# A SwiGLU feed-forward in token rows: stationary activations, streamed weights, and 32x32 turns before the down product

## The chip, the cores and the metric

The kernel runs on one core of a Trainium2 chip. The metric is the device time of one execution in microseconds; three runs of the kernel before took 2255.55, 2255.99 and 2256.78 us, so the median is 2255.99.

## The reference

One residual block on 256 tokens of width 2048, all in float32: a half-step feed-forward (FFN1), a token-mixing part (forgetting attention, differential attention, memory attention, merged by gates), and a second half-step feed-forward (FFN2). Each part has an RMSNorm in front and one behind. The change touches the two feed-forwards alone:

```python
def rmsnorm(x, g):
    y = x * lax.rsqrt(jnp.mean(x * x, axis=-1, keepdims=True) + EPS)
    return y * g

def swiglu(h, w_gate, w_up, w_down):          # h: 256 x 2048
    return (jax.nn.silu(h @ w_gate) * (h @ w_up)) @ w_down   # 2048 -> 5632 -> 2048

h = rmsnorm(x, ffn1_pre_g)
x = x + 0.5 * rmsnorm(swiglu(h, ffn1_w_gate, ffn1_w_up, ffn1_w_down), ffn1_post_g)
...  # token mixing
h = rmsnorm(x, ffn2_pre_g)
x = x + 0.5 * rmsnorm(swiglu(h, ffn2_w_gate, ffn2_w_up, ffn2_w_down), ffn2_post_g)
```

## The kernel before

**Split operands.** Each float32 operand of a large product is split into hi (rounded to the float32r format) and lo (what is left), and the product is taken as hi*hi + hi*lo + lo*hi. Activations are split once and kept as a tile with index (k, hi or lo, token), k counting slices of 128 rows. `rows_of` makes such tiles; its offset argument shifts the start by some elements. The factor of the norm per token is not applied to h: it is applied behind the product.

**The weight stream.** Class `Stream` lists all weight pieces of the kernel in the order of their use. A raw tile is 1 MB, loaded by one DMA on SP's queue (line 69), three raw buffers. Half of a raw tile is one piece; its hi comes from a ScalarE cast (line 92), its lo from a VectorE subtraction (line 93), into four split buffers. `ahead` splits as many pieces as there are free buffers, and issues the loads that follow; `take` hands out pieces (and splits them if nobody did so before); `release` gives their buffers back. The order of the instructions on each engine is the order of the program: nothing reorders it, so a wait holds up all that is behind it on that engine.

**Two forms of product.** `mm_a` (lines 206, 208) holds 128x128 blocks of weights stationary and streams activations: a matmul of 512 columns (hi weights against hi and lo of 256 tokens) and one of 256 (lo weights against hi). The result has FF features on partitions, and its two halves are added by `lr_sum` (lines 403, 405). `mm_b` (lines 247 to 249) holds 128x128 blocks of activations stationary and streams 512 columns of weights, three matmuls per slice and per token tile t of 128 tokens. The result has tokens on partitions.

**The feed-forward before.** `ffn_up` runs over 44 blocks m of 128 FF features. Block 0 takes gate and up together (`proj_a2`), with turns of later parts of x put in between; all others take `proj_a` for gate, then for up. Then the block is finished in eight to ten short instructions of 128x256: `lr_sum`, a multiplication by the row of token factors (`times_row`, a row that `row_of` spreads over the partitions), Silu, again the row, `lr_sum` of up, the product, and the split into `gh` (lines 282, 283), which is already in the layout that the down product wants as its stationary operand. The down product (`PostProj.body` and `last`) uses `proj_b`, which runs `mm_b` over pieces with two banks, one per token tile.

**PSUM.** Four banks are used in turn for products, four for transposes and attention.

**The ends of FFN1 and FFN2's beginning.** At the start x is loaded in four parts of 512 columns, each transposed on TensorE (`transpose_to`, lines 320 to 330), scaled by the norm's gain and split into `hT1`. Ahead of FFN2 the last product of the mixing part ends with token tile 0 first: with `lag=7` tile 0 is finished, x updated and turned (`x2_in`) while tile 1's last seven pieces run. Tile 1's update (line 397) and turns follow, and then FFN2's first block.

Of the kernel before, what the change touches and what calls it, by code (L numbers as in the profile page):

```python
# [16 lines left out]
P = 128  # L17
# [3 lines left out]
FF = 5632  # L21
FT = FF // P
NB = 428
NBS = 448
# [12 lines left out]
class Stream:  # L37
# [33 lines left out]
    def ahead(self, most=8):  # L71

        for _ in range(most):
            if self.done == len(self.plan):
                break
            _, r, half, extra = self.plan[self.done]
            if extra:
                if self.extra_pool is None:
                    break
                pool, tag = self.extra_pool, "x"  # L80
            else:
                if sum(not p[3] for p in self.plan[self.used:self.done]) == self.split_bufs:
# [8 lines left out]
            for i in range(2) if self.done == 0 else (slice(0, 2),):  # L91
# [24 lines left out]
def tile_block(ctx, tc, x, mem, f1gu, f1d, wqk, wv, wmkv, wgate, wbr, wout, f2gu, f2d,  # L116
# [21 lines left out]
    st = Stream(nc, rawp, splitp, 3, 4)  # L138
    st.add("gu1", f1gu[0, 0], f1gu[1, 0])
    for m in range(1, FT):  # L140
        st.add("gate1", f1gu[0, m])
        st.add("up1", f1gu[1, m])
    for i in range(4 * 11):
# [13 lines left out]
    for i in range(16):  # L157
        st.add("out", wout[i], extra={12: (1,), 13: (0, 1)}.get(i, ()))
    st.add("gu2", f2gu[0, 0], f2gu[1, 0])
    for m in range(1, FT):  # L160
        st.add("gate2", f2gu[0, m])
        st.add("up2", f2gu[1, m])
    for i in range(4 * 11):
# [46 lines left out]
    def new_bank(name):  # L210
        return mmp.tile([P, 512], F32, tag="mm", name=name)
# [12 lines left out]

    def proj_a2(name, act, inserts=()):

        banks = [new_bank("mm_a2") for _ in range(2)]
        inserts = dict(inserts)
        for half in range(2):
            ws = st.take(name, 2)  # L230
            for kk in range(8):
                k = half * 8 + kk
                inserts.get(k, lambda: None)()
                for i in range(2):
                    mm_a(banks[i], ws[i], kk, act, k, k == 0, k == KT - 1)
            st.release(2)
        return banks

    def mm_b(bank, piece, w, act, t, k0, start, stop):
# [10 lines left out]

    def proj_b(name, act, nk, w, banks=None, start=True, stop=True, lag=0, first_done=None, inserts=()):


        if banks is None:
            banks = [new_bank("mm_b") for _ in range(2)]
        pieces = nk // 2
        for i in range(pieces - lag):
            st.ahead()
            p, = st.take(name)
            for t in range(2):  # L260
                mm_b(banks[t], p, w, act, t, 2 * i, start and i == 0, stop and i == pieces - 1)
            st.release()
            fill()
        if lag:
# [12 lines left out]
        return banks  # L277

# [65 lines left out]
    class PostProj:  # L344
# [23 lines left out]

        def body(self):
            for n in range(3):  # L370
                banks = proj_b(self.name, self.act, self.nk, 512)
                for t in range(2):
                    self.evac(n, t, banks[t])
                self.load_g(n + 1)
# [39 lines left out]

    def ffn_up(idx, hT, stats, setup, inserts=()):

        first = []
        for m in range(FT):
            bu = None
            if m == 0:  # L420
                bg, bu = proj_a2(f"gu{idx}", hT, inserts)
                stats()
                first.append(proj_a(f"gate{idx}", hT))
                row, tp, gh = setup()
            else:
                bg = first.pop() if first else proj_a(f"gate{idx}", hT)
            ga = tp.tile([P, S], F32, tag="ga", name="ga", bufs=1)
            lr_sum(ga, bg, tp)
            times_row(ga, row)
            sg = tp.tile([P, S], F32, tag="sg", name="sg", bufs=1)  # L430
            nc.scalar.activation(out=sg, in_=ga, func=AF.Silu)
            times_row(sg, row)
            if bu is None:
                bu = proj_a(f"up{idx}", hT)
            up = tp.tile([P, S], F32, tag="ga", name="up", bufs=1)
            lr_sum(up, bu, tp)
            nc.vector.tensor_tensor(out=up, in0=sg, in1=up, op=ALU.mult)
            split_to(gh[:, m, 0], gh[:, m, 1], up)
        return gh

# [3 lines left out]
    hpool = h1_stack.enter_context(tc.tile_pool(name="hT1", bufs=1, side="right", reuse_waits="tile"))  # L444
    tp1 = h1_stack.enter_context(tc.tile_pool(name="ft1", bufs=1, side="right", reuse_waits="tile"))
    gp1 = g1_stack.enter_context(tc.tile_pool(name="gh1", bufs=1, side="left", reuse_waits="tile"))
    hT1 = rows_of(hpool, KT, OFF, name="hT1")
    gh1 = rows_of(gp1, FT, 0, name="gh1")
# [15 lines left out]
    def x_in(c):  # L464
        for t in range(2):
            transpose_to(hT1, chunk(x_sb, t, c), t, 4 * c, C_G1 + 4 * c, tp1)()

    x_in(0)
    st.ahead(2)

    xr = []
    ffn_up(1, hT1, lambda: xr.extend(token_rstd(x_sb, t) for t in range(2)), lambda: (row_of(xr, hpool), tp1, gh1),
           {1: lambda: x_in(1), 3: lambda: st.ahead(1), 5: lambda: x_in(2), 7: lambda: st.ahead(1),
            8: lambda: x_in(3), 10: lambda: st.ahead(2)})
    h1_stack.close()
# [427 lines left out]

    h3T = rows_of(h2p, KT, OFF, tag="h", name="h3T")
    fg_stack = ExitStack()
# [20 lines left out]
    post2.update(1, 1)  # L926
    splits = [x2_in(1, 0, 2), x2_in(1, 1)]

    def turn(c):
        splits.append(x2_in(1, c))  # L930

    splits.pop(0)()

    g2_stack, tp2_stack = ExitStack(), ExitStack()

    def setup2():
        row = row_of(h3r, h2p)
        fg_stack.close()
        mg_stack.close()
        yb_stack.close()  # L940
        tp = tp2_stack.enter_context(tc.tile_pool(name="ft2", bufs=1, side="left", reuse_waits="tile"))
        gp = g2_stack.enter_context(tc.tile_pool(name="gh2", bufs=1, side="right", reuse_waits="tile"))
        return row, tp, rows_of(gp, FT, 0, name="gh2")

    gh2 = ffn_up(2, h3T, lambda: h3r.extend(token_rstd(x_sb, t) for t in range(2)), setup2,
                 {1: lambda: (splits.pop(0)(), post2.update(1, 2), st.ahead(1)), 2: lambda: (turn(2), post2.update(1, 3)),
                  4: lambda: (splits.pop(0)(), st.ahead(1)), 5: lambda: turn(3), 8: lambda: splits.pop(0)(),
                  10: lambda: st.ahead(2)})
    tp2_stack.close()
    h2_stack.close()  # L950
    with tc.tile_pool(name="fg2", bufs=1, side="left", reuse_waits="tile") as fgp:
# [7 lines left out]

        post3.body()  # L960
        banks = post3.last(lag=4, first_done=lambda bank: finish(0, bank))
# [83 lines left out]
```

## Time and profile before

| what | value |
|---|---|
| median of three runs | 2255.99 us |
| the profiled execution | 2256.76 us |
| span of that execution, first to last instruction | 2255.0 us |
| TensorE (PE) busy | 99% |
| weight loads into TensorE (PEld) | 86% |
| VectorE (DVE) busy | 62% |
| ScalarE (ACT) busy | 49% |
| DMA engines, mean share of the main queue | 53.0% |
| mean granted TensorE clock | 0.998 |

A busy share is the time in which an engine had an instruction in it. Matmuls overlap in their ends, so the time from one start to the next is shorter than the duration that the profile gives: what a matmul costs in a stream is read from the starts.

### The profile page before, as it was taken

To read this page: it belongs to the slowest core of one execution; us is meant where nothing else is said; L and a number is where in the kernel's file an instruction comes from. 1 tells how busy PE (TensorE), PEld (TensorE's weight loads), DVE (VectorE), ACT (ScalarE), POOL (GpSimd) and SP (SyncE) were. 2 spreads that over 40 slices of the span, in tenths; PEclk is the share of its full clock that TensorE was granted. 3 is DMA by queue.
4 is the path that set the end of the run, shared out by engine and by line. 5 is a ranking of instruction groups with operands and counts; after the bars stand their busy time and mean duration, and the time that the engine had idled before them with its cause. 6 is when DMAs were issued, how large, how long until landed. Compare 5 with 4: busy or idle time off the path is not lost. (4 is left out here: it accounts for less than half of the span.)

```text
span 2255.0 us, 30353 instructions
## 1 busy us (share of the span) xinstructions
PE 2235.5 (99%) x12028; PEld 1947.3 (86%) x12028; DVE 1408.1 (62%) x1969; ACT 1097.8 (49%) x1704; POOL 11.3 (1%) x22
## 2 busy tenths in 40 slices
PE   8999999999999999999999999999999999999998
PEld 7888888888888898888888888878888888888887
DVE  6666666665444756766776767566666666664444
ACT  6444544445444654444555555456544445544433
POOL 0000000000000000000000000000000000000000
PEclk9999999999999999999999999999999999999999
DMA  6555555556555454544555555545555555555553
GB/s 226 190 194 194 189 187 187 190 192 229 191 202 199 171 190 148 180 144 159 174 181 205 176 199 187 208 154 197 187 187 189 192 194 191 187 199 203 192 202 138
DMA packets 63646, 423.15 MB, mean 188 GB/s; under 512 B 7440, under 2 KB 7824, under 8 KB 16144
## 3 DMA queue, kind: packets, MB, share of 16 engines
q1 hardware_dynamic: 59616, 415.33, 53.0%
q10 hardware_dynamic: 3888, 5.88, 0.8%
q8 instruction: 94, 1.54, 0.3%
q14 instruction: 48, 0.39, 0.1%
HBM read 419.09 MB, written 2.10 MB: 187 GB/s over the span
## 5 line engine op out<-in xcount | busy, mean ns | idle before, releaser
L93 DVE TENSOR_TENSOR lo<-raw,hi 128x1024 fp32r<-128x1024 f32 (+2 forms) x793 | 943.1, 1211 | 453.1 <-ACT hi L92 450.6
L92 ACT CAST hi<-raw 128x1024 fp32r<-128x1024 f32 (+2 forms) x793 | 808.7, 1037 | 382.3 <-PE mm_b L249 307.9
L206 PE MATMUL mm_a<-hT,hi 128*128 128x512 f32 x1408 | 490.7, 391 | 2.9 <-DVE hT L330 2.9
L206 PE MATMUL mm_a<-h3T,hi 128*128 128x512 f32 x1408 | 491.0, 392 | 1.0 <-DVE h3T L330 1.0
L208 PE MATMUL mm_a<-hT,lo 128*128 128x256 f32 x1408 | 398.3, 283 | 1.1 <-DVE lo L93 1.1
L208 PE MATMUL mm_a<-h3T,lo 128*128 128x256 f32 x1408 | 398.0, 283 | 0.0
L206 PE MATMUL mm_a<-h2T,hi 128*128 128x512 f32 x1088 | 384.0, 394 | 0.0
L206 PEld LDWEIGHTS mm_a<-hT,hi 128*128 128x128 f32 x1408 | 265.3, 188 | 58.8 <-ACT hi L92 3.5
L206 PEld LDWEIGHTS mm_a<-h3T,hi 128*128 128x128 f32 x1408 | 265.5, 189 | 56.8 <-ACT tg L322 1.2
L208 PE MATMUL mm_a<-h2T,lo 128*128 128x256 f32 x1088 | 306.5, 282 | 0.0
L403 ACT ACTIVATE left<-mm_a 128x256 f32<-128x256 f32 x244 | 93.5, 383 | 378.3 <-PE mm_a L208 378.3
L247 PE MATMUL mm_b<-hi,gh 128*128 128x512 f32 x704 | 274.2, 390 | 0.0
L249 PE MATMUL mm_b<-hi,gh 128*128 128x512 f32 x704 | 273.9, 389 | 0.0
L248 PE MATMUL mm_b<-lo,gh 128*128 128x512 f32 x704 | 273.9, 389 | 0.0
L208 PEld LDWEIGHTS mm_a<-hT,lo 128*128 128x128 f32 x1408 | 267.0, 190 | 2.5 <-DVE lo L93 2.5
L208 PEld LDWEIGHTS mm_a<-h3T,lo 128*128 128x128 f32 x1408 | 267.2, 190 | 0.0
L206 PEld LDWEIGHTS mm_a<-h2T,hi 128*128 128x128 f32 x1088 | 204.4, 188 | 41.9
L208 PEld LDWEIGHTS mm_a<-h2T,lo 128*128 128x128 f32 x1088 | 205.7, 189 | 0.2
L249 PEld LDWEIGHTS mm_b<-hi,gh 128*128 128x128 f32 x704 | 132.1, 188 | 27.6
L247 PEld LDWEIGHTS mm_b<-hi,gh 128*128 128x128 f32 x704 | 132.1, 188 | 27.4
L248 PEld LDWEIGHTS mm_b<-lo,gh 128*128 128x128 f32 x704 | 132.2, 188 | 27.1
L405 DVE TENSOR_TENSOR up<-mm_a,left 128x256 f32<-128x256 f32 x88 | 37.4, 424 | 71.4 <-ACT left L403 71.4
(205 smaller groups left out, 1779.5 us busy)
## 6 DMA issues: line engine op xcount, KB each, us to landing
raw<-in_f2gu SPq DMA_DIRECT2D x88, 1024.0 KB, 4.8
raw<-in_f1gu SPq DMA_DIRECT2D x86, 1024.0 KB, 4.8
raw<-in_wgate SPq DMA_DIRECT2D x48, 1024.0 KB, 4.7
raw<-in_f1d SPq DMA_DIRECT2D x44, 1024.0 KB, 4.8
raw<-in_f2d SPq DMA_DIRECT2D x44, 1024.0 KB, 4.7
raw<-in_wv SPq DMA_DIRECT2D x24, 856.0 KB, 4.5
raw<-in_wqk SPq DMA_DIRECT2D x20, 1024.0 KB, 4.8
raw<-in_wbr SPq DMA_DIRECT2D x16, 1024.0 KB, 4.7
```

Source lines behind the costliest of these rows:

```text
L92: self.nc.scalar.copy(out=hi[:, i], in_=src[:, i])
L93: self.nc.vector.tensor_tensor(out=lo[:, i], in0=src[:, i], in1=hi[:, i].bitcast(F32), op=ALU.subtract)
L206: nc.tensor.matmul(bank, lhsT=hi[:, i, c], rhs=act[:, k].rearrange("p s n -> p (s n)"), start=start, stop=False)
L208: nc.tensor.matmul(bank[:, 0:S], lhsT=lo[:, i, c], rhs=act[:, k, 0], start=False, stop=stop)
L247: nc.tensor.matmul(o, lhsT=xh, rhs=wh, start=start and kk == 0, stop=False)
L248: nc.tensor.matmul(o, lhsT=xh, rhs=wl, start=False, stop=False)
L249: nc.tensor.matmul(o, lhsT=xl, rhs=wh, start=False, stop=stop and kk == 1)
L403: nc.scalar.activation(out=left, in_=bank[:, 0:S], func=AF.Copy, scale=scale)
L405: nc.vector.tensor_tensor(out=dst, in0=bank[:, S:2 * S], in1=left, op=ALU.add)
```

## The change

The gate and up products of both feed-forwards take the form `mm_b`: activations stationary, weights streamed, in 11 blocks of 512 FF columns, the gate by `proj_b` (8 pieces), then the up by `proj_b`. Block 0 takes gate and up together in a new loop `proj_b2`, which goes through groups of pieces, first for token tile 0, then for tile 1, with the turns of x and the splits ahead put in as `inserts`. In FFN2 the first group has two pieces, so that tile 0 comes with both of them ahead of tile 1.

Behind it, a block is finished with tokens on partitions: Silu out of the gate bank with the token factor as its scale (ScalarE), product with the up bank (VectorE), a 32x32 turn on VectorE, per token tile. 16 DMAs of 32 partitions each (`regroup`) then bring the 32-blocks to the places that the down product wants, and 4 casts and 4 subtractions of 128x256 split them into `gh`. The DMAs are issued behind piece 1 of the next product, the split behind its piece 6. The order of the FF columns in the weight arrays is changed to match on the host's side of the layout (`_tiles_up`). The row of token factors, `lr_sum` and `times_row` are gone from the feed-forwards. The first two pieces of the kernel, in place of the first one, are split by halves. The offset of `hT1` and `h3T` becomes 0.

```diff
-    def ffn_up(idx, hT, stats, setup, inserts=()):
...
+    def proj_b2(name, act, groups, inserts):
+        banks = [[None, None], [None, None]]
+        for group in groups:
+            ws = {}
+            for t in range(2):
+                for i in group:
+                    inserts.get((i, t), lambda: None)()
+                    if t == 0:
+                        ws[i] = st.take(name, 2)
+                    for j in range(2):
+                        if i == 0:
+                            banks[j][t] = new_bank("mm_b2")
+                        mm_b(banks[j][t], ws[i][j], 512, act, t, 2 * i, i == 0, i == KT // 2 - 1)
+                    if t == 1:
+                        st.release(2)
+        return banks
...
+    def ffn_up(idx, hT, rstd, setup, groups, inserts):
+        state = {}
+        def gated(t, bank):
+            nc.scalar.activation(out=state["s"][:, t], in_=bank, func=AF.Silu, scale=rstd[t])
+        def product(t, bank):
+            sg = state["s"]
+            nc.vector.scalar_tensor_tensor(out=sg[:, t], in0=bank, scalar=rstd[t], in1=sg[:, t],
+                                           op0=ALU.mult, op1=ALU.mult)
+            nc.vector.transpose(out=state["z"][:, t], in_=sg[:, t])
+        def regroup():
+            for a in range(4):
+                for q in range(4):
+                    nc.sync.dma_start(out=state["w"][32 * q:32 * q + 32, :, a],
+                                      in_=state["z"][32 * a:32 * a + 32, :, P * q:P * (q + 1)])
+        def split(n):
+            src = state["w"].rearrange("p t a (k i) -> p k (t a) i", k=4)
+            hi, lo = (state["gh"][:, 4 * n:4 * n + 4, i].rearrange("p k (g i) -> p k g i", i=32) for i in range(2))
+            for k in range(4):
+                split_to(hi[:, k], lo[:, k], src[:, k])
+        def open_block():
+            for name, shape in (("s", [P, 2, 512]), ("z", [P, 2, 512]), ("w", [P, 2, 4, P])):
+                state[name] = state["tp"].tile(shape, F32, tag="f" + name, name="f" + name, bufs=1)
+        late = {}
+        for n in range(FB):
+            if n == 0:
+                bg, bu = proj_b2(f"gu{idx}", hT, groups, inserts)
+                state["tp"], state["gh"] = setup()
+                open_block()
+                for t in range(2):
+                    gated(t, bg[t])
             else:
+                bg = proj_b(f"gate{idx}", hT, KT, 512, steps=late)
+                open_block()
+                for t in range(2):
+                    gated(t, bg[t])
+                bu = proj_b(f"up{idx}", hT, KT, 512)
+            for t in range(2):
+                product(t, bu[t])
+            late = {1: regroup, 6: lambda n=n: split(n)}
+        return state["gh"], late
...
+    def setup1():
+        x_r.extend(token_rstd(x_sb, t) for t in range(2))
+        return tp1, gh1
+
+    _, late1 = ffn_up(1, hT1, x_r, setup1, [[i] for i in range(8)],
+                      {(0, 1): lambda: (st.ahead(2), x_in(1)), (1, 1): lambda: st.ahead(2), (2, 0): lambda: x_in(2),
+                       (2, 1): lambda: st.ahead(2), (3, 1): lambda: st.ahead(2), (4, 0): lambda: x_in(3),
+                       (4, 1): lambda: st.ahead(2), (5, 1): lambda: st.ahead(2), (6, 1): lambda: st.ahead(2)})
...
-    post1.body()
+    post1.body(late1)
...
+    gh2, late2 = ffn_up(2, h3T, h3r, setup2, [[0, 1]] + [[i] for i in range(2, 8)],
+                        {(1, 0): lambda: x2_in(1, 0)(), (0, 1): lambda: (post2.update(1, 2), x2_in(1, 1)()),
+                         (1, 1): lambda: (post2.update(1, 3), st.ahead(2), x2_in(1, 2)()),
+                         (2, 1): lambda: (st.ahead(2), x2_in(1, 3)()), (3, 1): lambda: st.ahead(2),
+                         (4, 1): lambda: st.ahead(2), (5, 1): lambda: st.ahead(2), (6, 1): lambda: st.ahead(2)})
...
+def _tiles_up(w):
+    k, m = w.shape
+    return _tiles_b(w.reshape(k, m // 512, 4, 4, 32).transpose(0, 1, 3, 2, 4).reshape(k, m), 512)
```

## Rows read from the trace of the kernel before

**Rows 1.** The page: span, engines' busy us and share, the chain by engine.
```profile
span 2255.0 us, 30353 instructions
...
PE 2235.5 (99%) x12028; PEld 1947.3 (86%) x12028; DVE 1408.1 (62%) x1969; ACT 1097.8 (49%) x1704; POOL 11.3 (1%) x22
...
PE 32%; issue 0%; DVE 0%; POOL 0%; ACT 0%; DVEq 0%; POOLq 0%; ACTq 0%
```
**Rows 2.** Windows, FFN1 gate/up: length, busy by engine, clock, DMA share, GB/s.
```profile
9.30:506.00 496.70, 495.29 (x2845) 438.20 (x2845) 328.40 (x457) 253.13 (x393) 1.11 (x2) 1.00 0.57 193
```
**Rows 3.** Timeline, TensorE in gate/up: start, duration; first and last of 98.
```profile
199.89 0.39 PE L206 MATMUL mm_a<-hT,hi 128*128 128x512 f32 x1
...
233.52 0.39 PE L206 MATMUL mm_a<-hT,hi 128*128 128x512 f32 x1
```
**Rows 4.** Timeline, TensorE in the down product; first and last of 60.
```profile
599.65 0.39 PE L247 MATMUL mm_b<-hi,gh 128*128 128x512 f32 x1
...
639.77 0.39 PE L247 MATMUL mm_b<-hi,gh 128*128 128x512 f32 x1
```
**Rows 5.** Timeline, entry of FFN1, and the first matmul of its down product.
```profile
9.11 2.42 DVE L93 TENSOR_TENSOR lo<-raw,hi 128x512 fp32r<-128x512 f32 x3
...
9.34 0.76 PE L206 MATMUL mm_a<-hT,hi 128*128 128x512 f32 x1 [2.66 <-DVE hT L330]
...
506.00 0.39 PE L247 MATMUL mm_b<-hi,gh 128*128 128x512 f32 x1
```
**Rows 6.** Timeline, entry of FFN2, and the first matmul of its down product.
```profile
1509.18 2.35 DVE L93 TENSOR_TENSOR lo<-raw,hi 128x1024 fp32r<-128x1024 f32 x2
...
1510.46 0.39 PE L249 MATMUL mm_b<-hi,mT 128*128 128x512 f32 x1
...
1513.41 1.29 PE L320 MATMUL tr_h<-ident,x_sb 128*128 128x128 f32 x8 [2.55 <-DVE x_sb L397]
...
1515.68 0.77 PE L206 MATMUL mm_a<-h3T,hi 128*128 128x512 f32 x1 [0.98 <-DVE h3T L330]
...
2008.02 0.39 PE L247 MATMUL mm_b<-hi,gh 128*128 128x512 f32 x1
```
**Rows 7.** Windows, the start of FFN2; the clock stands behind POOL.
```profile
1514.90:1521.60 6.70, 5.92 (x20) 5.15 (x21) 5.68 (x11) 4.40 (x12) 0.00 (x0) 0.50 0.18 43
```
**Rows 8.** Groups by line and form: count | busy us, mean ns of one | idle.
```profile
L93 DVE TENSOR_TENSOR lo<-raw,hi 128x1024 fp32r<-128x1024 f32 x743 | 891.6, 1223 | 418.3 <-ACT hi L92 416.0
...
L437 DVE TENSOR_TENSOR up<-sg,up 128x256 f32<-128x256 f32 x88 | 37.5, 426 | 3.0
...
L397 DVE SCALAR_TENSOR_TENSOR x_sb<-fg,rstd_post,x_sb 128x512 f32<-128x512 f32 x24 | 17.1, 747 | 0.5
...
L812 DVE COPY pt_m<-tr_pm 128x512 f32<-128x512 f32 x4 | 2.8, 692 | 2.8 <-PE tr_pm L810 2.8
...
L674 DVE COPY f<-fb 32x256 bf16<-32x256 bf16 x3 | 0.7, 217 | 0.1
...
L92 ACT CAST hi<-raw 128x1024 fp32r<-128x1024 f32 x743 | 764.5, 1046 | 351.5 <-PE mm_b L249 277.1 <-PE mm_a L206 38.3 <-PE mm_br L206 21.3
...
L303 ACT ACTIVATE junk<-x_sb 128x512 bf16<-128x512 f32 x24 | 15.3, 636 | 0.6
...
L303 ACT ACTIVATION_READ_ACCUMULATOR junk<-x_sb 128x1 f32 x24 | 4.6, 192 | 0.0
...
L431 ACT ACT_TABLE_LOAD x1 | 1.3, 1283 | 0.0
```
**Rows 9.** DMA issues: queue, count, KB each, median us from issue to landing.
```profile
raw<-in_f1gu SPq DMA_DIRECT2D x86, 1024.0 KB, 4.8
...
out<-x_sb SPq DMA_DIRECT2D x8, 256.0 KB, 2.1
```
**Rows 10.** Waits of SP's queue: waiter, for what, us in total, times, longest.
```profile
SPq L452 <- DMA raw<-in_f1gu: 1.3, 2, 1.0
```
**Rows 11.** Line 69 on SP: count, ns of an issue (min/median/max), first and last start.
```profile
L69 SPq DMA_DIRECT2D raw<-in_f1gu x86: 327/328/328, 8.9 to 482.5; - x86
```

More of the change, by code (lines that the diff above doesn't have):

```diff
@@ L22 @@
 FT = FF // P
+FB = FF // 512
 NB = 428
@@ L90, in ahead @@
                       .rearrange("p (k n) -> p k n", k=2)[:, :, 0:w] for t in ("hi", "lo"))
-            for i in range(2) if self.done == 0 else (slice(0, 2),):
+            for i in range(2) if self.done < 2 else (slice(0, 2),):
                 self.nc.scalar.copy(out=hi[:, i], in_=src[:, i])
@@ L138, in tile_block, with add_up @@
     st = Stream(nc, rawp, splitp, 3, 4)
[L139 to L142, printed above, removed]
+    def add_up(idx, w):
+        for i in range(4):
+            st.add(f"gu{idx}", w[0, i], w[1, i])
+        for n in range(1, FB):
+            for j, name in enumerate(("gate", "up")):
+                for i in range(4):
+                    st.add(f"{name}{idx}", w[j, 4 * n + i])
+    add_up(1, f1gu)
     for i in range(4 * 11):
@@ L158, in tile_block @@
         st.add("out", wout[i], extra={12: (1,), 13: (0, 1)}.get(i, ()))
[L159 to L162, printed above, removed]
+    add_up(2, f2gu)
     for i in range(4 * 11):
@@ L223, in proj_a @@
         return bank
[L225 to L237, printed above, removed]
     def mm_b(bank, piece, w, act, t, k0, start, stop):
@@ L249, in mm_b, with proj_b @@
             nc.tensor.matmul(o, lhsT=xl, rhs=wh, start=False, stop=stop and kk == 1)
-    def proj_b(name, act, nk, w, banks=None, start=True, stop=True, lag=0, first_done=None, inserts=()):
+    def proj_b(name, act, nk, w, banks=None, start=True, stop=True, lag=0, first_done=None, inserts=(), steps=()):
+        steps = dict(steps)
         if banks is None:
@@ L263, in proj_b @@
             fill()
+            steps.get(i, lambda: None)()
         if lag:
@@ L412, in times_row @@
             nc.vector.tensor_tensor(out=dst, in0=dst, in1=row, op=ALU.mult)
-    def ffn_up(idx, hT, stats, setup, inserts=()):
[L417 to L424, printed above, removed]
-            else:
[L426 to L439, printed above, removed]
+    def ffn_up(idx, hT, rstd, setup, groups, inserts):
[28 more added lines that the diff above has]
+                    gated(t, bg[t])
+            else:
+                bg = proj_b(f"gate{idx}", hT, KT, 512, steps=late)
[7 more added lines that the diff above has]
+        return state["gh"], late
@@ L444, in tile_block @@
     hpool = h1_stack.enter_context(tc.tile_pool(name="hT1", bufs=1, side="right", reuse_waits="tile"))
-    tp1 = h1_stack.enter_context(tc.tile_pool(name="ft1", bufs=1, side="right", reuse_waits="tile"))
     gp1 = g1_stack.enter_context(tc.tile_pool(name="gh1", bufs=1, side="left", reuse_waits="tile"))
-    hT1 = rows_of(hpool, KT, OFF, name="hT1")
+    tp1 = g1_stack.enter_context(tc.tile_pool(name="ft1", bufs=1, side="left", reuse_waits="tile"))
+    hT1 = rows_of(hpool, KT, 0, name="hT1")
     gh1 = rows_of(gp1, FT, 0, name="gh1")
@@ L465, in x_in @@
         for t in range(2):
-            transpose_to(hT1, chunk(x_sb, t, c), t, 4 * c, C_G1 + 4 * c, tp1)()
+            transpose_to(hT1, chunk(x_sb, t, c), t, 4 * c, C_G1 + 4 * c, hpool)()
     x_in(0)
     st.ahead(2)
[L471 to L474, printed above, removed]
+    x_r = []
+    def setup1():
[5 more added lines that the diff above has]
+                       (4, 1): lambda: st.ahead(2), (5, 1): lambda: st.ahead(2), (6, 1): lambda: st.ahead(2)})
     h1_stack.close()
@@ L926, in tile_block @@
     post2.update(1, 1)
[L927 to L934, printed above, removed]
+    g2_stack = ExitStack()
     def setup2():
-        row = row_of(h3r, h2p)
+        h3r.extend(token_rstd(x_sb, t) for t in range(2))
         fg_stack.close()
@@ L940, in setup2 @@
         yb_stack.close()
-        tp = tp2_stack.enter_context(tc.tile_pool(name="ft2", bufs=1, side="left", reuse_waits="tile"))
         gp = g2_stack.enter_context(tc.tile_pool(name="gh2", bufs=1, side="right", reuse_waits="tile"))
[L943 to L949, printed above, removed]
+        tp = g2_stack.enter_context(tc.tile_pool(name="ft2", bufs=1, side="right", reuse_waits="tile"))
+        return tp, rows_of(gp, FT, 0, name="gh2")
+    gh2, late2 = ffn_up(2, h3T, h3r, setup2, [[0, 1]] + [[i] for i in range(2, 8)],
[3 more added lines that the diff above has]
+                         (4, 1): lambda: st.ahead(2), (5, 1): lambda: st.ahead(2), (6, 1): lambda: st.ahead(2)})
     h2_stack.close()
```

12 lines of the change are left out of this document (6 added, 6 removed).

## The prediction

> **What bounds the kernel now.** I read the page first: TensorE is busy 99% of a 2255.0 us span, and the chain that ended last is TensorE with next to no other engine [rows 1]. The reader is to see that nothing but TensorE's own stream can shorten this kernel, so the question is what one unit of the gate and up work costs on TensorE in the old and the new form, and where TensorE stands still. Then I read stretches: the FFN1 gate/up stretch runs from 9.34 to 506.00 us, TensorE full in it, VectorE at 66% and ScalarE at 51% [rows 2, 5]. Then the timeline inside both for the start-to-start time of matmuls [rows 3, 4], and last the two places where TensorE waits: the entry of FFN1 [rows 5] and of FFN2 [rows 6].
>
> **The steady part: the same columns in fewer matmuls.** A unit is 128 weight columns of one 128-row slice for 256 tokens. Old form (mm_a): one matmul of 512 columns and one of 256. 97 such pairs lie between 199.89 and 233.52 us [rows 3]: 33.63/97 = 346.7 ns a unit. New form (mm_b, as the down product has it): 6 matmuls of 512 columns for 4 units, that is 1.5 a unit. 59 groups of three lie between 599.65 and 639.77 [rows 4]: 40.12/59 = 680 ns, 226.7 ns a matmul, 340.0 ns a unit. Both stream 768 columns a unit; the gain is half a matmul's overhead, 6.7 ns. There are 44 x 2 x 16 = 1408 units in each FFN, 2816 in all: **-18.8 us**. The lower bound of the gain is mm_b at mm_a's mean of 346.7/768 = 0.451 ns a column, which is no gain at all; the upper bound is the 226.7 read. I take 226.7, since the new loop has the down product's operands: 512 moving columns of hi or lo, 128 stationary columns.
> The Trainium skill, "TensorE: Matmul & The Clock Gate", section "Back-to-back issue gap", gives 2.5 ns of fixed cost a matmul above N/2.4. Half of that on 2816 units would be an estimated 3.6 us in place of 18.8. The rows show 226.7 ns for 512 columns, 13 ns above 213.3, so here the trace differs from the page and the sum goes by the trace.
>
> **What lies beside it.** Per block of 512 FF columns the change takes 24 instructions of 256 columns from VectorE (six per 128 FF columns, 0.425 us each [rows 8], 10.2 us) and puts in 2 products (like the 512-wide scalar_tensor_tensor, 0.75 us), 2 turns and 4 subtractions of 0.425. ScalarE loses 16 short ones and gets 2 Silus and 4 casts. No row shows a 32x32 turn: the nearest below is an instruction of 256 columns at 0.43, above it sixteen short 32-partition copies of 0.217 each, one per column of blocks, 3.5; I take 0.7, the 512-wide copy out of PSUM [rows 8]. So 2.9 us of VectorE at the end of a block. Three split pieces of weights are ahead then, 3 x 12 x 0.2267 = 8.2 us of TensorE, and the next split (1.05 ScalarE, 1.22 VectorE [rows 8]) is done about 3.7 us after the block's end T. Cost at the 20 ordinary seams: nothing; the cover is gone only if a turn takes over about 3 us.
>
> **The new DMAs.** Sixteen of 32 KB per block on SP's queue, 352 in all, put behind the weight load of piece 0 and in front of that of piece 2. They wait for the turns (T+2.5); SP is there at about T+3.4, when it has issued a weight load. An issue costs 0.33 us [rows 11]. Two x loads at the start waited for landings of weight loads that they have nothing to do with [rows 10]; in program order those stand eight DMAs earlier, so I count eight in flight: seven go out by T+5.7, the eighth waits for the weight load before it (4.8 us [rows 9], T+8.2), the rest are out by T+11.2 and landed by about T+14. The split that reads them stands behind piece 6, which ScalarE reaches at T+17. The next weight load goes out some 2.5 us later than it could; its first half is wanted at T+19 and lands at T+16. Cost: nothing. What is queued behind: all weight loads (below as a rival).
>
> **Entry of FFN1.** Before, 496.66 us less 1408 x 0.3467 = 488.1 leaves 8.5 us, that is, a virtual start at 17.9. Of that, the first matmul waited for both token tiles to be split (9.34), the first ones ran at 0.76 instead of 0.39 us, and more were held up by lo's and turns (all four small matmuls that spread the row of norms are in it too). After: the first matmul needs tile 0 alone and starts near 8.6; its second waits for the first lo (9.11 + 0.7 = 9.8); then two pieces of six matmuls at the slow pace of about 0.43 us end at 14.6, eight transposes follow (1.29 us in the other entry [rows 6], about 1.5 here), then tile 1's twelve to 18.7. 24 x 0.2267 = 5.4, so 13.3 lost up to here; 16 more transposes and their gaps, 2.1: virtual start 15.4. **-2.5 us** (bounds -5 with the fast pace from 13 us on, +1 if it comes 3.5 us late).
>
> **Entry of FFN2.** Before: the last product of the mix starts at 1510.46, the first of FFN2 at 1515.68, and the stretch ends at 2008.02: 2008.02 - 1510.69 - 488.1 = 9.2 lost, among it 6.8 us at half clock [rows 6, 7]. After: tile 0's first pieces need nothing of tile 1; their lo is ready at 1511.5 [rows 6], so 12 matmuls run 1510.7 to 1513.4. Then come the four transposes of tile 1 (the first two of x's four parts are updated by 1513.4 already now), to 1513.9. Piece 1 is split only behind that turn: ScalarE 1515.2 to 1516.2, VectorE casts and subtracts until 1516.3, then lo at 1517.5 and 1518.7. So TensorE stands from 1513.9 to 1517.5 but for one matmul; the rest runs on: 48 matmuls (10.9 us) done at 1526.5, 4.9 lost, and 0.5 for the last transposes: 5.4. **-3.8 us** (bounds -6 and -0.5).
>
> **A new stall after block 0.** In both FFNs the first block's last group is split early, and nothing splits ahead for block 1: that split stands behind eight squares (0.64 us and 0.19 for the read-out [rows 8]), two Silus (0.6), two products and two turns. With T the end of block 0: the buffers of its last early split come free two groups ahead, at T-10.9, so ScalarE is through it at T-8.8 and through the squares at T-2.2; the second Silu waits for its power on POOL and ends at T-0.5; then hi of the next piece to T+0.55. VectorE: second product 0.17 to 0.92 behind up's last matmul, turn to 1.6, lo to 2.8. TensorE does one matmul and waits to T+2.9: 2.7 us. FFN2 also loads the Silu table before it (a ScalarE row of this kernel has 1.28 [rows 8]), which moves this to about 3.1. **+5.8 us** (bounds: turn at 0.43, +5.2; turn at 3.5, 7.5 + 7.9 = +15).
>
> **Sum.** -18.8 - 2.5 - 3.8 + 5.8 = -19.3: the span 2255.0 becomes 2235.7. The profiled execution took 2256.76 us, 1.76 outside the span, so 2237.5; the median of the runs, 2255.99, is 0.77 below that execution: **2236.7 us**.
>
> **Rivals.**
> (1) The clock falls in the new stalls. For it: at FFN2's entry, 4.8 us without a product matmul were followed by 6.8 us at a granted clock of 0.50, 1.2 in place of 2.4 GHz [rows 6, 7], about 3.4 us lost. Against: the new stalls are at most 2.3 us on either side of a lone matmul. One to three falls: 2240 to 2247. Chance 0.17. The same page of the Trainium skill, section "Why this matters for your kernels", asks that matmul bursts follow each other without long idle gaps, or the clock falls; the trace's 4.8 us agrees, and no row has a gap near 2.3.
> (2) The turn is far dearer than a copy: at 3.5 us VectorE is 2 x 0.75 + 7.0 past each block's end, its lo comes at T+9.3 against 8.2 of cover, 1.1 us x 20, and the first seams cost 9.6 more: -19.3 + 22 + 9.6 = +12, 2268. Halfway (about 3 us) it is even. Chance 0.06.
> (3) The other sign: the sixteen DMAs land one after the other and hold SP's queue. The price of one is then its landing, 2.1 us for the lightest row [rows 9]: 33.6 us a block. The next weight load goes out at T+37, lands and is split by T+44; TensorE wants it at T+27.2. 17 us x 22 blocks: about 2600. It decides from 1.05 us each: (27.2 - 2.3 - 4.8 - 3.4)/16. Against it speak the waits that reach eight back [rows 10]. Chance 0.09. The Trainium skill, "DMA: Bandwidth & Descriptors", section "Rules for kernel authors", calls transfers under 64 KB mostly overhead; that is this rival's side, and no row here has a 32 KB transfer between two SBUF tiles.
> (4) The form gains little: mm_b in this place at 0.451 ns a column, -0.5 in all, 2255. Chance 0.05. By the 2.5 ns of the Trainium skill's page on TensorE above it would be an estimated 2252.
>
> **How the numbers follow.** The forecast has 0.63, 2236.7, with its own range 2230 to 2243 from the bounds of the entries. The range reaches down to 2228 (-18.8 - 5 - 6 + 5.2 = -24.6, and 2-3 us for what I have not seen) and up to 2251, which takes in (1) and part of (4), 0.63 + 0.17 + some of the rest. A measurement of this kernel tells 0.2%, 4.5 us. Faster: the forecast, (1) and a part of (2), 0.82. Same: most of (4), half of (2), 0.08. Slower: (3) and the far end of (2), 0.10.
>
> **What would show it.** Three matmuls every 680 ns in the gate/up stretches; each gate/up stretch, from its first matmul to the first of the down product, near 488 us in FFN1 (now 496.7); no TensorE gap at ordinary block seams; one gap of 2 to 3 us some 43 us behind the start of each FFN; SP waits on landings of the small DMAs, but no TensorE wait on weights. Wrong would be a gate/up cadence of 228 ns or more, gaps at every 43.5 us, or clock falls after block 0.

## The result, and the profile after

The changed kernel takes 2241.76 us (median of 4 runs, 2241.23 to 2242.72) against 2255.96 before (4 runs): ratio 0.9937, 95% interval 0.992 to 0.9954. It is 0.6% faster; 2236.7 was predicted, within 2228 to 2251. The miss is 5.1 us, and the terms of the sum show where it lies. In the profiled executions the span went from 2255.0 to 2239.4:

| term | predicted, us | read from the two traces, us |
|---|---|---|
| steady gate/up work | -18.8 | -18.8 |
| entry of FFN1 | -2.5 | -2.5 |
| entry of FFN2 | -3.8 | -0.9 |
| stall behind block 0, both FFNs | +5.8 | +5.6 |
| from the last matmul to the end | 0 | +1.0 |
| span | -19.3 | -15.6 |

The other 1.3 us of the miss lie outside the span's terms: the profiled execution of before was 0.8 us above the median of its runs (the prediction's sum took that off), that of after, 2241.23, is 0.5 below its own. The row on FFN2's entry compares one execution with one: run 9, a second execution of the kernel before, lost 7.9 us there and not 9.2, so the before side of this row alone moves by 1.3 us.

First two rows of the page and the FFN1 gate/up window (columns as in [rows 1, 2]). TensorE is as full as before; VectorE and ScalarE have less to do.

```profile
span 2239.4 us, 27119 instructions
...
PE 2216.1 (99%) x10612; PEld 1873.1 (84%) x10612; DVE 1286.2 (57%) x1616; ACT 1037.0 (46%) x1483; POOL 11.3 (1%) x22
```
```profile
8.69:496.98 488.29, 485.50 (x2137) 401.11 (x2138) 265.99 (x279) 222.62 (x282) 1.11 (x2) 1.00 0.59 208
```

The steady part, in the timeline of TensorE (start, duration of one; the distance of starts counts). 59 groups of three lie between these two rows, 40.12 us, 680.0 ns a group: what the down product showed in [rows 4], where the old form had 346.7 x 2 = 693.4 for the same work [rows 3].

```profile
199.82 0.39 PE L236 MATMUL mm_b<-hi,hT 128*128 128x512 f32 x1
...
239.94 0.39 PE L236 MATMUL mm_b<-hi,hT 128*128 128x512 f32 x1
```

Entry of FFN1, answering [rows 5]: the first matmul, the second that waits for lo, and the first of the down product. The stretch has 2112 matmuls, and at 0.22667 they are 478.72 us; 496.98 - 478.72 - 2.81 (the stall below) puts the virtual start, the time at which a stream without a gap would have begun, at 15.45, where 15.4 was predicted.

```profile
8.69 0.79 PE L236 MATMUL mm_b<-hi,hT 128*128 128x512 f32 x1 [1.92 <-ACT hi L93]
10.01 0.79 PE L237 MATMUL mm_b<-lo,hT 128*128 128x512 f32 x1 [0.52 <-DVE lo L94]
...
496.98 0.39 PE L236 MATMUL mm_b<-hi,gh 128*128 128x512 f32 x1
```

The seam behind block 0 of FFN1 (the place where block 1's matmuls follow block 0's): TensorE, then ScalarE and VectorE. The splits come one behind the other when the squares, Silus, products and turns are through: hi from 58.43, lo from 60.63.

```profile
58.72 0.39 PE L238 MATMUL mm_b<-hi,hT 128*128 128x512 f32 x1
59.52 0.50 PE L236 MATMUL mm_b<-hi,hT 128*128 128x512 f32 x1 [0.41 <-ACT hi L93]
61.87 0.50 PE L237 MATMUL mm_b<-lo,hT 128*128 128x512 f32 x1 [1.85 <-DVE lo L94]
62.21 0.40 PE L238 MATMUL mm_b<-hi,hT 128*128 128x512 f32 x1
```
```profile
58.43 3.88 ACT L93 CAST hi<-raw 128x1024 fp32r<-128x1024 f32 x4
```
```profile
60.00 0.71 DVE L437 STREAM_TRANSPOSE fz<-fs 128x512 f32<-128x512 f32 x1
60.63 4.59 DVE L94 TENSOR_TENSOR lo<-raw,hi 128x1024 fp32r<-128x1024 f32 x4
```

Three steps from one start to the next take 0.80, 2.35 and 0.34 instead of 0.227 each, 2.81 us more; FFN2's seam has the same steps. No other block seam has a gap.

Entry of FFN2, answering [rows 6, 7]: timeline, then the window of the half clock (the clock stands behind POOL, 0.50).

```profile
1501.40 0.39 PE L238 MATMUL mm_b<-hi,mT 128*128 128x512 f32 x1
1501.63 0.39 PE L236 MATMUL mm_b<-hi,h3T 128*128 128x512 f32 x1
...
1504.35 0.60 PE L330 MATMUL tr_h<-ident,x_sb 128*128 128x128 f32 x4
1507.17 0.49 PE L236 MATMUL mm_b<-hi,h3T 128*128 128x512 f32 x1 [2.22 <-ACT hi L93]
1508.56 0.80 PE L237 MATMUL mm_b<-lo,h3T 128*128 128x512 f32 x1 [0.90 <-DVE lo L94]
...
1991.43 0.39 PE L236 MATMUL mm_b<-hi,gh 128*128 128x512 f32 x1
```
```profile
1507.60:1514.40 6.80, 5.90 (x17) 4.68 (x17) 2.70 (x3) 0.46 (x1) 0.00 (x0) 0.50 0.73 255
```

The first product starts right behind the last of the mix, as forecast. Lost: 1991.43 - 1501.63 - 478.72 - 2.81 = 8.3 us, against 9.2 before and 5.4 forecast.

The new operations, for [rows 8, 9, 11]: groups by line, an issue on SP (min/median/max), issue to landing and one block's sixteen.

```profile
L437 DVE STREAM_TRANSPOSE fz<-fs 128x512 f32<-128x512 f32 x44 | 31.3, 712 | 1.5
```
```profile
L443 SPq DMA_DIRECT2D fw<-fz x352: 585/595/1616, 65.6 to 2005.5; - x176
...
DMA to landing us min/median/max: 1.8/2.0/6.7
```
```profile
109.38 11.37 SPq L443 DMA_DIRECT2D fw<-fz  x16
```

### The profile page after: what moved, and what is told of

Same layout as the page of the kernel before. It is cut to its first block, busy times and chain, and to the rows that moved or that the text cites. A ratio compares the mean times of both kernels' runs of the same rounds, so it can differ in the third digit from the quotient of the medians.

```text
span 2239.4 us, 27119 instructions
## 1 busy us (share of the span) xinstructions
PE 2216.1 (99%) x10612; PEld 1873.1 (84%) x10612; DVE 1286.2 (57%) x1616; ACT 1037.0 (46%) x1483; POOL 11.3 (1%) x22
## 5 line engine op out<-in xcount | busy, mean ns | idle before, releaser
L94 DVE TENSOR_TENSOR lo<-raw,hi 128x1024 fp32r<-128x1024 f32 (+2 forms) x794 | 956.9, 1211 | 776.9 <-ACT hi L93 773.8
L236 PE MATMUL mm_b<-hi,h3T 128*128 128x512 f32 x704 | 275.2, 391 | 2.6 <-ACT hi L93 2.6
L237 PE MATMUL mm_b<-lo,h3T 128*128 128x512 f32 x704 | 275.1, 391 | 2.7 <-DVE lo L94 2.7
L236 PE MATMUL mm_b<-hi,hT 128*128 128x512 f32 x704 | 275.4, 391 | 2.3 <-ACT hi L93 2.3
L237 PE MATMUL mm_b<-lo,hT 128*128 128x512 f32 x704 | 275.1, 391 | 2.4 <-DVE lo L94 2.4
L238 PE MATMUL mm_b<-hi,hT 128*128 128x512 f32 x704 | 274.9, 390 | 0.0
L238 PE MATMUL mm_b<-hi,h3T 128*128 128x512 f32 x704 | 274.9, 390 | 0.0
L236 PEld LDWEIGHTS mm_b<-hi,h3T 128*128 128x128 f32 x704 | 132.7, 189 | 30.9 <-ACT hi L93 3.3
L237 PEld LDWEIGHTS mm_b<-lo,h3T 128*128 128x128 f32 x704 | 132.7, 189 | 30.8 <-DVE lo L94 3.4
L237 PEld LDWEIGHTS mm_b<-lo,hT 128*128 128x128 f32 x704 | 132.7, 188 | 30.9 <-DVE lo L94 3.2
L236 PEld LDWEIGHTS mm_b<-hi,hT 128*128 128x128 f32 x704 | 132.7, 188 | 30.5 <-ACT hi L93 3.2
L238 PEld LDWEIGHTS mm_b<-hi,hT 128*128 128x128 f32 x704 | 132.7, 189 | 27.5
L238 PEld LDWEIGHTS mm_b<-hi,h3T 128*128 128x128 f32 x704 | 132.7, 189 | 27.4
L238 PEld LDWEIGHTS mm_b<-hi,gh 128*128 128x128 f32 x704 | 132.1, 188 | 27.7
```

Source lines behind the costliest of these rows:

```text
L236: nc.tensor.matmul(o, lhsT=xh, rhs=wh, start=start and kk == 0, stop=False)
L237: nc.tensor.matmul(o, lhsT=xh, rhs=wl, start=False, stop=False)
L238: nc.tensor.matmul(o, lhsT=xl, rhs=wh, start=False, stop=stop and kk == 1)
```

## The experiments

Where a kernel was run more than once its median is given; the kernel before took 2256.03 to 2256.15 beside them.

**1. The seam's stall taken away.** In both FFNs the squares go in front of pieces 5 and 6, and two more pieces are split ahead:

```
-                        (4, 1): lambda: st.ahead(2), (5, 1): lambda: st.ahead(2), (6, 1): lambda: st.ahead(2)})
+                        (4, 1): lambda: st.ahead(2), (5, 0): lambda: x_r.append(token_rstd(x_sb, 0)),
+                        (5, 1): lambda: st.ahead(2), (6, 0): lambda: x_r.append(token_rstd(x_sb, 1)),
+                        (6, 1): lambda: st.ahead(2), (7, 1): lambda: st.ahead(2)})
```

> The changed kernel, but the squares that give the norm of each token tile are taken earlier: tile 0's ahead of piece 5 and tile 1's ahead of piece 6 of block 0 (before: both behind block 0), and two more weight pieces are split ahead behind tile 1's piece 7, so that block 1 finds its first pieces split. In both FFNs. Theory: the stall of 2.81 us behind block 0 (0.80 and 2.35 us, less the 0.34 of two regular steps) is ScalarE's order of work alone, so both stalls go: 2 x -2.81, 2241.8 becomes about 2236.1, and no TensorE start-to-start time over 0.45 us stands at that seam. Rival: the next pieces' weights or the split buffers are not there any earlier, and the stall only moves into the new split: within 1 us of 2241.8.

Measured: 2233.63 us, ratio to before 0.9903 (0.9888 to 0.9918), 8.1 us under the changed kernel. In the timeline of TensorE the seam is gone, every step 0.227:

```profile
58.40 0.39 PE L238 MATMUL mm_b<-hi,hT 128*128 128x512 f32 x1
58.62 0.39 PE L236 MATMUL mm_b<-hi,hT 128*128 128x512 f32 x1
```

So the stall was the order of work, as the theory has it. The profile also has 8 slow matmuls at FFN1's entry instead of 12 (1.7 us) and half the time at half clock in FFN2 (1.1 us); 5.6 + 2.8 = 8.4 is its span's difference, 2239.4 to 2231.0. The 2.8 are not what the edit is for: run 7, of the changed kernel without it, has 8 slow matmuls there as well, and run 6 has 3.4 us at half clock at FFN2's entry. Three of the four executions lie 2.3 to 3.3 us under the expected 2236.1, though, so whether chance alone gave the 2.8 stays open.

**2. FFN2's second pieces split earlier,** one line between the updates of token tile 0 and tile 1:

```
     post2.update(1, 0)
+    st.ahead(2)
     post2.update(1, 1)
```

> The changed kernel, but at FFN2's entry the second weight pieces are split between the two updates of x's chunk 0 (token tile 0 and tile 1), ahead of tile 1's turn instead of behind it. Theory: the idle of 2.2 + 0.9 us before the second pieces is this order alone, and the 6.8 us at a granted clock of 0.50 behind it is its consequence: the entry loses about 2.5 us in place of 8.27, 2241.8 becomes about 2236, and the granted clock shows no 0.50 in that stretch. Rival: the clock falls there whatever the idle is (the half-clock stretch stays): only about 2 us are won, 2239 to 2240. Second rival: tile 1's update and turn, which now stand behind the split, come late themselves: no gain, 2241 to 2243.

Measured: 2236.45 us, ratio 0.9914 (0.9899 to 0.9929), 5.3 under the changed kernel. The stall is down to one step of 0.68 and the half clock at the entry is gone (timeline, then windows: the entry at a clock of 1.00; a stretch behind FFN2's seam at 0.50).

```profile
1504.17 0.48 PE L236 MATMUL mm_b<-hi,h3T 128*128 128x512 f32 x1
1504.85 0.50 PE L237 MATMUL mm_b<-lo,h3T 128*128 128x512 f32 x1 [0.20 <-DVE lo L94]
```
```profile
1501.09:1508.00 6.91, 6.71 (x34) 5.33 (x33) 6.67 (x10) 3.71 (x8) 0.56 (x1) 1.00 0.30 95
1551.10:1554.49 3.39, 3.39 (x10) 2.62 (x9) 2.22 (x2) 0.34 (x1) 0.00 (x0) 0.50 0.69 222
```

The entry loses 2.4 us instead of 8.3 (1986.67 to the down product - 1501.09 - 478.72 - 2.81 = 4.05, of which 1.7 is the 3.4 us at half clock behind the seam; run 10, without that stretch at FFN2's seam, gives 2.45 directly). Both rivals fall: with the idle gone the clock doesn't fall at the entry. The stretch behind the seam was new, after steps (0.80 and 2.35 us) which had caused none in the changed kernel's profile.

**3. Both edits.**

> The two edits before together: the earlier squares with the added split at both seams, and the earlier split at FFN2's entry. Theory: the two act in different places and add up: -5.6 and about -5.8, 2241.8 becomes about 2230.4. Rival: they share the work that covers them (in FFN2 the squares then stand behind pieces that are already late), and FFN2's seam stall comes back: 2233 or more.

Measured: 2229.27 us, ratio 0.9883 (0.9866 to 0.9899): 12.5 under the changed kernel, where 11.4 was expected. Between the two entries and the end no clock fall is left; TensorE's waits are those of FFN1's entry (4.7, 1.9 and 0.5) and 0.2 us at FFN2's:

```profile
PE tr_h L330 <- DMA ident<-in_cf: 4.7, 1, 4.7
PE mm_b L236 <- ACT hi L93: 1.9, 1, 1.9
PE mm_b L237 <- DVE lo L94: 0.7, 2, 0.5
```

**4. The number of matmuls put back.** The product on the weights' low part is cut in two; columns and operands stay:

```
+            for c in (slice(0, 256), slice(256, 512)) if halve[0] else (slice(0, w),):
+                nc.tensor.matmul(bank[:, c], lhsT=xh, rhs=wl[:, c], start=False, stop=False)
```

> The changed kernel with the second of the three products of each 512-column group in the gate and up products (the one on the weights' low part) cut into two matmuls of 256 columns. The columns are the same, the matmuls of four units are 8 instead of 6, as many as in the form before. Theory: the steady gain is half a matmul's fixed cost a unit, 13.3 ns a matmul above its columns at 2.4 GHz; then the group goes from 680 ns to 693.3, 2816/2 = 1408 more matmuls for each token tile and 2816 in all put back 2816/2 x 13.3 = 18.8 us: about 2260.5. Rival: the gain comes from the operands' roles (activations stationary, weights moving) and not from the count: 2242, cadence 680 ns. Second rival: a matmul of 256 columns can't hide its weight load, which then shows: more than 2270.

(The text's "2816 in all" miscounts: there are 22 x 64 = 1408 groups, so 1408 more matmuls; 1408 x 13.3 = 18.8 stands.) Measured: 2265.67 us, ratio 1.0042 (1.0027 to 1.0057), 23.9 more than the changed kernel and slower than before. Timeline of TensorE; the group goes from 680 to about 697 ns (545 groups take 379.69 us between 100 and 480 us, 696.7 each):

```profile
199.95 0.40 PE L240 MATMUL mm_b<-lo,hT 128*128 128x256 f32 x2
200.18 0.40 PE L241 MATMUL mm_b<-hi,hT 128*128 128x512 f32 x1
200.41 0.40 PE L238 MATMUL mm_b<-hi,hT 128*128 128x512 f32 x1
200.65 0.39 PE L240 MATMUL mm_b<-lo,hT 128*128 128x256 f32 x2
```

An extra matmul with the same columns costs 16.7 ns; 1408 of them are 23.5 us. The count of matmuls alone gives back the whole steady gain and more; the operands' roles by themselves saved nothing that this run could see. The size was expected at 13.3; why it is 16.7 stays open. Each matmul here brings its own weight load (12020 of each in this run, 10612 of each in the changed kernel), so the run doesn't tell a matmul's own cost from that of its load. The Trainium skill, "TensorE: Matmul & The Clock Gate", section "Back-to-back issue gap", gives 2.5 ns above N/2.4 for the gap of an isolated matmul; the trace differs here too.

**5. The small DMAs doubled:** behind each DMA into w a second one of the same rows into s, which is dead by then.

```
+                    nc.sync.dma_start(out=state["s"][32 * q:32 * q + 32, :, P * a:P * (a + 1)],
+                                      in_=state["z"][32 * a:32 * a + 32, :, P * q:P * (q + 1)])
```

> The changed kernel with each of the sixteen small DMAs of a block issued twice, the second time into the tile s, which nothing reads after its turn: 32 of 32 KB per block on SP's queue, 704 in all. Theory: in the changed kernel the sixteen take 11.4 us of SP from first to last, so 32 take about 22 to 23 us; SP waits for free weight buffers for most of its time, and the prediction's own limit for them was 1.05 us x 16 = 16.8 us a block. By that limit the next weight load is 5 to 6 us late at each of 21 seams: 110 to 130 us more, about 2360. Rival: the limit was worked out too tight, since the small DMAs are issued while weight loads already ahead in the ring cover the time, and the second sixteen are not waited for by anyone: 2242 to 2246. Second rival: the split of the turned block is late for nobody but the loads share the DMA engines: weights land later, a few scattered gaps, 2246 to 2260.

Measured: 2407.64 us, ratio 1.0671 (1.064 to 1.0702), 166 more. SP's queue in block 1 (first and last of the 32, then the next weight loads), and TensorE:

```profile
65.37 0.74 SPq L443 DMA_DIRECT2D fw<-fz  x1
...
86.66 0.60 SPq L445 DMA_DIRECT2D fs<-fz  x1
87.36 1.48 SPq L70 DMA_DIRECT2D raw<-in_f1gu  x3
```
```profile
88.46 0.39 PE L238 MATMUL mm_b<-hi,hT 128*128 128x512 f32 x1
93.52 0.79 PE L236 MATMUL mm_b<-hi,hT 128*128 128x512 f32 x1 [4.66 <-ACT hi L93]
94.78 0.79 PE L237 MATMUL mm_b<-lo,hT 128*128 128x512 f32 x1 [0.47 <-DVE lo L94]
```

The 32 hold SP for 21.9 us, 5.1 over the prediction's limit of 16.8, and TensorE idles 4.66 + 0.47 = 5.1. So the limit of rival (3) was right: the sixteen of the change, 11.4 us, are hidden with some 5 us to spare. The total came out above 110 to 130 because there are 22 such seams, not 21, and the clock falls in the idle: at this seam it stands at 0.50 from 90.90 to 97.70 us, and TensorE works in 3.7 of these 6.8 us. 166/22 = 7.5 us a seam.

The same profile holds a case that bears on run 2. The order of work at FFN2's entry is that of the changed kernel, and so is the idle, but the clock doesn't fall (timeline, then window, at a clock of 1.00):

```profile
1589.86 0.49 PE L236 MATMUL mm_b<-hi,h3T 128*128 128x512 f32 x1 [2.22 <-ACT hi L93]
1591.25 0.50 PE L237 MATMUL mm_b<-lo,h3T 128*128 128x512 f32 x1 [0.89 <-DVE lo L94]
```
```profile
1592.00:1596.00 4.00, 4.00 (x21) 3.27 (x21) 1.26 (x3) 1.24 (x5) 0.00 (x0) 1.00 0.99 342
```

**6. A dear turn made real:** each turn five times over, so 3.7 us instead of 0.71.

```
+            for _ in range(5):
+                nc.vector.transpose(out=state["z"][:, t], in_=sg[:, t])
```

> The changed kernel with each turn of a 128x512 block on VectorE done five times over (the same result): 8 x 0.712 = 5.7 us more on VectorE behind each block. This is the prediction's case of a dear turn (3.5 us) made real: it expected 1.1 us more at each of 20 ordinary seams and 9.6 us at the two first ones, 32 us in all, about 2273 here. Rival: the three pieces that are split ahead cover more than 8.2 us, for TensorE still has matmuls of the block's last pieces when VectorE begins: only the two first seams grow, by 5.7 each, about 2253. Second rival: the small DMAs go out 5.7 us later and hold the weight loads at a worse time: over 2280.

Measured: 2286.82 us, ratio 1.0136 (1.0106 to 1.0165), 45 more. The first seam and an ordinary one:

```profile
59.13 0.50 PE L236 MATMUL mm_b<-hi,hT 128*128 128x512 f32 x1 [0.42 <-ACT hi L93]
66.11 0.79 PE L237 MATMUL mm_b<-lo,hT 128*128 128x512 f32 x1 [6.48 <-DVE lo L94]
```
```profile
119.48 0.39 PE L236 MATMUL mm_b<-hi,hT 128*128 128x512 f32 x1
121.03 0.50 PE L237 MATMUL mm_b<-lo,hT 128*128 128x512 f32 x1 [1.16 <-DVE lo L94]
```

An ordinary seam's gap is 1.3 us (1.55 - 0.23) where 1.1 was expected, so the cover of 8.2 us was about right. The total is 13 us over the expected 32: from seam to seam it is 45.0 us (eight blocks from 119.48 to 479.67), 1.5 over 192 x 0.22667 = 43.5, which makes 8 us in 20 blocks; at the first seam of FFN1 the clock falls in the idle, and TensorE works at half clock from 66.11 to about 69.8 us, at that of FFN2 likewise; and FFN2 has four steps of 1.0 to 1.3 us in mid-block. At the first of these (1745.86 us) the cast of the weights had waited 2.40 us for a weight load to land, so loads come late there, as the second rival has it; why in these four blocks alone stays open.

**7 and 8. The changed kernel twice more; 10. the kernel of run 2 once more.** No edit, one execution each.

> The changed kernel once more, for a second profiled execution. The first showed 6.83 us at a granted clock of 0.50 at FFN2's entry and none at the two seams behind block 0, although the seams' idle (0.80 and 2.35 us between starts) was the same in the kernel with FFN2's entry mended, where 3.41 us at 0.50 followed one of them. Theory: whether the clock falls behind such a short idle, and for how long, differs between executions of one kernel; the long idle at FFN2's entry makes it fall in every one. Then this profile shows 3.4 or 6.8 us at 0.50 at FFN2's entry, and perhaps a stretch at a seam. Rival: the fall belongs to the order of instructions, and this profile shows the same stretches as the first.

> The changed kernel a third time, as the run before: by the theory a fall at FFN2's entry again (3.4 or 6.8 us), and at the seams none or 3.4 us; span 2238 to 2242 by what falls there are. By the rival exactly the stretches of the first profile.

> The kernel with FFN2's second pieces split earlier once more: the idle of 0.80 and 2.35 us at both seams stands. Theory: the half-clock stretch of 3.41 us behind FFN2's seam was this execution's; here it may stand at either seam, at both or at none, and FFN2's entry shows none again. Rival: the same stretch at the same place.

Measured: 2241.14, 2240.89 and 2235.74 us. Windows of run 7, of run 8 and of run 10 (FFN1's seam, then FFN2's entry):

```profile
60.32:63.70 3.38, 3.38 (x9) 2.60 (x9) 3.13 (x3) 0.21 (x1) 0.00 (x0) 0.50 0.40 107
...
1507.55:1514.38 6.83, 5.96 (x16) 4.81 (x17) 2.61 (x3) 0.37 (x1) 0.00 (x0) 0.50 0.74 266
```
```profile
60.30:63.70 3.40, 2.12 (x9) 1.78 (x10) 3.40 (x4) 1.72 (x2) 0.00 (x0) 1.00 0.14 19
1507.14:1513.97 6.83, 6.04 (x17) 4.51 (x16) 2.89 (x3) 0.65 (x1) 0.00 (x0) 0.50 0.69 247
```
```profile
61.42:64.82 3.40, 3.40 (x10) 2.64 (x9) 2.51 (x3) 0.00 (x0) 0.00 (x0) 0.50 0.58 195
1501.95:1509.00 7.05, 6.84 (x34) 5.43 (x33) 6.81 (x10) 3.72 (x8) 0.56 (x1) 1.00 0.33 103
```

The fall at FFN2's entry stands in all three profiles of the changed kernel and in none of the four with the entry mended (runs 2, 3, 10 and 11). The falls behind the seams come and go between executions of one kernel: one in three profiles of the changed kernel, at FFN2's seam in run 2 and at FFN1's in run 10. For the seams the theory holds. For the entry it says too much when it has the fall in every execution: of the four other profiles with the unmended entry, run 4 shows the long stretch, runs 1 and 6 one of 3.4 us, and run 5 none. The idle is what lets the clock fall there; whether it falls, and for how long, differs between executions here too. FFN1's entry differs too: full clock comes back after 12 slow matmuls in the first profile and after 8 in run 7. The Trainium skill, "TensorE: Matmul & The Clock Gate", section "What's actually happening", says that the slow start differs from run to run of one kernel; the trace agrees. A seam with a fall costs 1.7 us more.

**9. The kernel before once more,** for the last microsecond.

> The kernel before once more. The changed kernel's tail, from the last matmul's start to the end of the span, was 8.45 us against 7.43 before, as the last output's landing was waited for 2.7 us instead of 1.6. Theory: that is a difference between executions and not the change's, for no edit touches the tail; the tail here is anywhere from 7.4 to 8.9 us. Rival: the tail of this kernel is 7.4 us again, and the change (tiles in other places, queues in another state) costs 1 us there. The half-clock stretch at FFN2's entry shows again, 3.4 or 6.8 us.

Measured: 2255.82 us. The half clock at FFN2's entry lasted half as long as in [rows 7] (window, 0.50; from 1519.3 us on the clock is 1.00):

```profile
1515.80:1519.20 3.40, 3.16 (x11) 2.78 (x12) 3.20 (x7) 1.79 (x5) 0.00 (x0) 0.50 0.02 5
```

From the last matmul's start to the end it is 7.8 us in both profiles of before (last output's wait 1.6) and 8.8 to 8.9 in all three of the changed kernel (2.6 to 2.7). So the theory fell: the microsecond is no chance of an execution. Looking for what differs in the last 7 us, I found one packet of an instruction queue (q14) in the changed kernel, and none in the kernel before. Runs 5 and 6, of the new form too, have none either, and their tails are 7.9 and 8.0 us. The row of the changed kernel:

```profile
q14 instruction: 1, 0.01, 0.6%
```

**11. VectorE's instruction stream made longer,** on the kernel of run 3, by 176 one-column writes.

```
+            for _ in range(8):
+                nc.vector.memset(state["z"][:, 0, 0:1], 0.0)
```

> The kernel with both edits and, behind each split of a turned block, 8 one-column writes on VectorE (into z, which nothing reads any more; 176 in all, beside a TensorE that is busy). In every profile of the new form but two a packet of the instruction queue (q14) stands in the last 4 us, and the last output's landing is waited for 2.6 to 2.7 us; in the kernel before (twice), in the one with repeated turns and in the one with doubled DMAs no such packet stands there, and from the last matmul's start to the span's end it is 7.8 to 8.0 us in place of 8.8 to 8.9. Theory: the 1 us of the tail is that packet, and it goes by the length of an engine's instruction stream; with VectorE's longer by 176, as with the repeated turns, the packet moves out of the tail and the kernel takes about 2228.3, tail 7.8 to 8.0. Rival: the tail is the new form's and the packet only stands beside it: 2229.3, tail 8.8, whether the packet is there or not.

Measured: 2228.03 us, ratio 0.9876 (0.986 to 0.9893), the fastest of all. Its tail is 7.95 us (8.9 in run 3), the last output's wait 1.7, and no instruction packet stands in it. The theory's numbers came; that the packet delays the landing, and not something else that the stream's length moves, is the likely reading and not shown step by step.

## Why the prediction was right or wrong

**Steady part: right, to 0.1 us.** The cadence taken from the down product held, and run 4 shows that its reason, the cost of a matmul (with its weight load) beyond its columns, is what pays. Rival (4) is out. One slip beside the sum: half of 2.5 ns on 2816 units is 3.5 us, not 3.6.

**Beside it: right.** The turn took 0.712 us (0.7 assumed), and run 6 confirms the cover of 8.2 us: 1.3 to 1.5 us a seam for 1.1. Rival (2)'s threshold of about 3 us fits that, and the rival didn't happen.

**The new DMAs: nothing lost, as forecast, though an issue was mis-sized.** An issue took 0.595 us instead of 0.33, so the sixteen end some 15.5 us behind the block's end (120.75, block 1 ending at 105.3), not at 11.2; with 2.0 us to land they come at about 17.5, as ScalarE gets to the split that reads them (122.77). The eighth did wait for a weight load, as I had counted, but for some 0.5 us and not 2.5 (SP's waits there are 5.4 us in ten blocks of FFN1). The three microseconds of slack I counted there weren't there. The weight loads had theirs: run 5 puts rival (3)'s limit where the prediction had it.

**Entry of FFN1: right** in two of three profiles (virtual start 15.4 and, in run 8, 496.69 - 481.53 = 15.2; run 7 has 13.6, 1.7 earlier, which its fall at the seam takes back): that the slow pace lasted through all twelve first matmuls, as the term assumed, differs between executions, so hitting it to 0.1 us was in part luck. **Stall behind block 0: right,** 2.81 for 2.7, and 2.81 for 3.1: the Silu table load in FFN2 was hidden.

**Entry of FFN2: the step that failed,** 2.9 us short. The order of work came as written: the lone matmul and the stall, lo at 1508.56 where the forecast, moved by the earlier start (9.06 us), has 1508.4. What I left out of the term is what rival (1) says: the term lets "the rest" of the 48 matmuls behind the stall run on at full speed, and the first eleven of them ran at 427 ns. The clock was 0.50 for 6.8 us; TensorE was busy in 5.9 of them, so 2.9 us were lost, the whole shortfall of the term. I had set this aside because the new stalls were "at most 2.3 us on either side of a lone matmul" and "no row has a gap near 2.3". That misread my own rows: the 4.8 us before the old fall were no single idle but 2.55 us before eight transposes and 0.98 behind them [rows 6], much like the 2.22 and 0.90 around a lone matmul that came. Run 2 shows that without the idle the clock stays up, run 5 that the same idle doesn't always bring it down. So rival (1) was right at one of its places. Its lower end, 2240, is nearer to the runs than the forecast, but in part by luck: the fall cost 2.9 us, not 3.4, and the end, which it doesn't name, added 1.0. In the profile of after, the seams, which it named too, stayed at full clock.

**The end: a term that I didn't have,** 1.0 us, which goes with the instruction packet (runs 9 and 11); that the packet causes it is not shown. The last 1.3 us of the miss are the two profiled executions against their medians.

## What to carry to other kernels

Where TensorE is full, count matmuls, each with its weight load, and not only columns: the same columns in three quarters of the matmuls was worth 18.8 us here, and cutting one in three in half cost 23.5. A new block order must be looked at in its first seam, where nothing has been split ahead, since a stall of 2 to 3 us can cost its length again in half-clock time; putting the squares earlier and two splits ahead there and at FFN2's entry won 12.5 us, nearly as much as the change itself. A queue that also carries the weights has a limit that can be worked out beforehand: time from the last load ahead to its use, less landing and split.

## What the runs showed of the hardware that I had not expected

- At full clock a 512-column matmul of this kind takes 226.7 ns, 13.3 above 512/2.4, which [rows 4] had shown; at half clock 427, which is 512/1.2 with nothing above it. Cutting one of three in two costs 16.7 ns (run 4).
- The same idle (steps of 0.80 and 2.35 us around a lone matmul) is followed by 3.4 us at half clock in some executions of a kernel and by none in others. The longer idle of FFN2's entry (2.22 and 0.90 us around one) was followed by 6.8 us in four profiles, by 3.4 in two and by none in one.
- A DMA of 32 KB from 32 partitions to 32 others takes 0.595 us of SP's queue to issue and 2.0 to land; a weight load of 1 MB is issued in 0.33 [rows 11].
- 176 idle writes on VectorE went with a tail 1.0 us shorter (8.9 to 7.95).
